# Eight stores of the folded value/output weights, issued from POOL instead of SP

## The chip, the cores and the metric

The kernel runs on one core of one Trainium2 chip. The metric is the device time of one execution in microseconds (us). Besides the timed runs there is one profiled execution, with every instruction and every DMA on record; all quoted rows of the profile come from it. PE is the tensor engine, DVE the vector engine, ACT the scalar engine, POOL the GpSimd engine and SP the sync engine, which here does nothing but issue DMAs.

## The reference

One layer of a streaming encoder on x (2048 tokens x 1024) and mem (256 memory tokens x 1024), all in float32. Cut to what matters:

```python
u = rms_norm(h, g_mix_pre);  z = u @ w_in                  # split into 7 column groups
y = concatenate([swa_with_sinks(...), hgrn2(...)]) @ w_out  # window attention | gated recurrence
h = h + rms_norm(y, g_mix_post)
u = rms_norm(h, g_x_pre);  m = rms_norm(mem, g_mem)
y = cross_attention(u, m, wq_x, wk_x, wv_x, wo_x)           # 4 heads of 256, 256 memory tokens
h = h + rms_norm(y, g_x_post)
u = rms_norm(h, g_ffn_pre)
y = (silu(u @ w_gate) * (u @ w_up)) @ w_down                # 1024 -> 2816 -> 1024
h = h + rms_norm(y, g_ffn_post)
```

## The kernel before

The work runs in three stages, each with pools of its own in SBUF and PSUM.

**Stage 1** projects the first half of the tokens. **Stage 2** projects the second half and runs the window attention and the recurrence. Beside its last part runs `fold_cross` (L285), which folds the cross-attention weights: since the memory is fixed, `wq_x` and the keys are multiplied into one matrix `qk_d`, and the values and `wo_x` into one matrix `vo_d` (1024 x 1024, in DRAM). **Stage 3** (`phases`, L1191) is one long chain of blocked products: the output projection, the scores (with `qk_d`), the values (with `vo_d`), the FFN.

Every product is made in float32 from two halves, "hi" (a rounded copy) and "lo" (the rest), in three matmuls per pair: hi x hi, hi x lo, lo x hi. In stage 3 these are lines L1110, L1111 and L1112, on tiles `S` (stationary, 128x512) and `T` (moving, 128x512 per slice). An `S` tile is made from a raw tile `sraw` that a DMA has loaded: ACT or POOL writes hi (L974, L976), DVE writes lo (L977). Seven products stand in for eight (a Strassen scheme), so DVE also forms sums of raw tiles (`sum`, L1079).

**The end of the fold** is where the change lies (L346 to L369). For each head `h` two tiles of `wo_x` are loaded (`raw`, by SP), split by ACT (`whi`, L150) and DVE (`wlo`, L153), and multiplied on PE (L359 to L361) into four PSUM banks. Then, for each of two row blocks, ACT copies one bank (L366) and DVE another (L367) into the two halves of a row tile `o`, and `o` is stored to `vo_d`: 8 stores of 128x1024 float32, 512 KB each. The tiles `o` come in turn from tag `x` (3 buffers) and tag `z` (2 buffers) of the pool `io` (L61), so the third `z` tile takes the place of the first once that one's store has read it, and the fourth `x` tile that of the first. The names in the rows below are `x_7948`, `x_7996`, `x_8044`, `x_8092` and `z_7952`, `z_8000`, `z_8048`, `z_8096`, in program order.

**What sets the order.** Each engine executes its own instructions strictly in order, and so does each DMA-issuing sequencer: an instruction that waits for a semaphore holds up all that stand behind it on that engine. The order itself is written by a planner at build time, from the program text and its own costs. SP issues nearly all loads and stores, `store` (L77) among them. `store_late` (L80) issues a store from POOL instead; before the change only four stores of stage 1 use it (L652). POOL also issues the accumulating loads of stage 3 (`add`, L1480) and makes some hi halves. The first loads of stage 3 (`sraw` from `y_d`, the output of the two mixers) stand in SP's order behind the stores of the fold.

Of the kernel before, what the change touches and what calls it, by code (L numbers as in the profile page):

```python
# [18 lines left out]
P = 128  # L19
# [29 lines left out]
class Layer:  # L49
# [86 lines left out]
    def raw_tile(self):  # L136
        self._n += 1
        return self.wp.tile([P, D], F32, tag="raw", name=f"raw_{self._n}", bufs=3)

    def split_tiles(self):  # L140
        self._n += 1
        hi = self.wp.tile([P, D], F32R, tag="hi", name=f"whi_{self._n}", bufs=3)
        lo = self.wp.tile([P, D], F32R, tag="lo", name=f"wlo_{self._n}", bufs=3)
        return hi, lo
# [140 lines left out]
    def fold_cross(self):  # L285
# [32 lines left out]
        for d in (0, 4, 1, 5, 2, 6, 3, 7):  # L318
            th, tl = self.wcols(self.I["wq_x"], d, "A")
            o = self.io_tile("x")  # L320
            for q in range(2):
                ps = self.bank("sh"[q])
                for r in range(2):
                    h = 2 * q + r
# [21 lines left out]
        for h in range(4):  # L346
            banks = [[self.bank(k) for k in "sh"] for _ in range(2)]
            for i in range(2):
                j = 2 * h + i
                raw = raw_tile()  # L350
                self.load(raw, self.I["wo_x"][j * P:(j + 1) * P, :])
                wh, wl = split_tiles()
                self.split(raw, wh, wl, "A")
                for mt in range(2):
                    ms = slice(mt * P, (mt + 1) * P)
                    ah, al = vT[0][:, j, ms], vT[1][:, j, ms]
                    for q in range(2):
                        sl = slice(q * 512, (q + 1) * 512)
                        nc.tensor.matmul(banks[mt][q], ah, wh[:, sl], start=(i == 0), stop=False)  # L359
                        nc.tensor.matmul(banks[mt][q], ah, wl[:, sl], start=False, stop=False)  # L360
                        nc.tensor.matmul(banks[mt][q], al, wh[:, sl], start=False, stop=(i == 1))  # L361
                if i == 0:
                    yield
            for mt in range(2):
                o = self.io_tile("xz"[mt])
                nc.scalar.activation(o[:, 0:512], banks[mt][0], AF.Copy)  # L366
                nc.vector.tensor_copy(o[:, 512:D], banks[mt][1])  # L367
                self.store(self.vo_d[(2 * h + mt) * P:(2 * h + mt + 1) * P, :], o)
            yield  # L369


# [1403 lines left out]
```

## Time and profile before

| what | value |
|---|---|
| median of 3 runs | 2562.99 us (2562.63 to 2563.87) |
| profiled execution, its own time | 2559.88 us |
| its span, from the first to the last instruction | 2558.2 us |
| PE busy | 2510.6 us, 98% of the span |
| DVE, ACT, POOL busy | 1758.5, 1248.5, 457.1 us |
| mean clock granted to PE | 0.995 of full speed |
| loads and stores issued by SP (queue q1) | 443.76 MB, 51.7% of the 16 DMA engines' span |
| DMAs issued by POOL (queue q0) | 40.90 MB, 8.4% |
| stores to `vo_d`, issued by SP | 8, between 751.3 and 770.5 us |

How to read the rows: a timeline row has the start in us, the duration, the engine, the line, the operation, output<-input, and in brackets the idle time before it and what ended that. "SPq" is a DMA being issued by SP; the transfer itself comes after it, and "DMA to landing" is the time from issue to the last byte. The windows view has a row per stretch of time: length, busy us of each engine with its count of instructions, the granted clock, the share of the 16 DMA engines in use, and GB/s. A matmul's shown duration is longer than the distance to the next one, since matmuls overlap: the distance from start to start is what counts. Some matmul records are missing from the trace.

### The profile page before, as it was taken

To read this page: it belongs to the slowest core of one execution; us is meant where nothing else is said; L and a number is where in the kernel's file an instruction comes from. 1 tells how busy PE (TensorE), PEld (TensorE's weight loads), DVE (VectorE), ACT (ScalarE), POOL (GpSimd) and SP (SyncE) were. 2 spreads that over 40 slices of the span, in tenths; PEclk is the share of its full clock that TensorE was granted. 3 is DMA by queue.
4 is the path that set the end of the run, shared out by engine and by line. 5 is a ranking of instruction groups with operands and counts; after the bars stand their busy time and mean duration, and the time that the engine had idled before them with its cause. 6 is when DMAs were issued, how large, how long until landed. Compare 5 with 4: busy or idle time off the path is not lost. (4 is left out here: it accounts for less than half of the span.)

```text
span 2558.2 us, 34111 instructions
## 1 busy us (share of the span) xinstructions
PE 2510.6 (98%) x12012; PEld 2095.5 (82%) x12012; DVE 1758.5 (69%) x2813; ACT 1248.5 (49%) x2606; POOL 457.1 (18%) x633
## 2 busy tenths in 40 slices
PE   8999999999998999999999999999999999999998
PEld 7777888887997888888788888888888888888886
DVE  6868587788667578787876555585566666664756
ACT  5454365656654566565554333353333344543543
POOL 2233343222312343224210000000000000000022
PEclk9999999999999999999999999999999999999999
DMA  6254545466986796868973542254555433566798
GB/s 239 98 207 138 174 144 159 152 201 191 286 302 194 229 278 204 278 208 223 312 247 115 181 157 75 93 187 140 181 192 187 165 129 137 202 212 189 228 223 208
DMA packets 269386, 489.97 MB, mean 192 GB/s; under 512 B 20640, under 2 KB 127136, under 8 KB 268704
## 3 DMA queue, kind: packets, MB, share of 16 engines
q1 hardware_dynamic: 256832, 443.76, 51.7%
q0 software_dynamic: 11232, 40.90, 8.4%
q10 hardware_dynamic: 1152, 3.15, 0.3%
q8 instruction: 94, 1.54, 0.2%
q14 instruction: 76, 0.62, 0.1%
HBM read 326.26 MB, written 161.48 MB: 191 GB/s over the span
## 5 line engine op out<-in xcount | busy, mean ns | idle before, releaser
L1110 PE MATMUL psm<-T,S 128*128 128x512 f32 x2744 | 1065.3, 392 | 18.5 <-ACT S L974 9.7
L1111 PE MATMUL psm<-T,S 128*128 128x512 f32 x2744 | 1072.8, 391 | 0.0
L1112 PE MATMUL psm<-T,S 128*128 128x512 f32 x2744 | 1066.0, 391 | 1.9 <-DVE S L977 1.8
L1110 PEld LDWEIGHTS psm<-T,S 128*128 128x128 f32 x2744 | 517.1, 188 | 129.9 <-ACT S L974 10.5
L1112 PEld LDWEIGHTS psm<-T,S 128*128 128x128 f32 x2744 | 516.8, 188 | 111.3 <-DVE S L977 3.7
L1111 PEld LDWEIGHTS psm<-T,S 128*128 128x128 f32 x2744 | 517.2, 188 | 106.4
L974 ACT ACTIVATE S<-sum 128x512 fp32r<-128x512 f32 (+1 forms) x336 | 206.0, 617 | 328.1 <-PE psm L1112 325.0
L977 DVE TENSOR_TENSOR S<-sraw,S 128x512 fp32r<-128x512 f32 (+1 forms) x312 | 211.7, 686 | 218.2 <-ACT S L974 201.8
L977 DVE TENSOR_TENSOR S<-sum,S 128x512 fp32r<-128x512 f32 (+1 forms) x400 | 273.0, 687 | 79.2 <-ACT S L974 64.1
L1125 ACT ACTIVATE part<-psm 128x512 f32<-128x512 f32 x294 | 173.2, 592 | 181.9 <-PE psm L1112 180.8
L974 ACT ACTIVATE S<-sraw 128x512 fp32r<-128x512 f32 (+1 forms) x271 | 165.9, 617 | 168.6 <-PE psm L1112 144.4
L1482 POOL DMA_DIRECT2D row<-y_d x28 | 25.0, 893 | 1070.9 <-DMA sraw<-hid_d 905.3
L1453 ACT ACTIVATE junk<-row 128x512 f32<-128x512 f32 x160 | 99.6, 625 | 97.0 <-DVE row L1475 33.6
L170 PE MATMUL psg<-u,whi 128*128 128x512 f32 x352 | 142.7, 406 | 3.9 <-DVE z L696 2.1
L977 DVE TENSOR_TENSOR T<-row,T 128x1024 fp32r<-128x1024 f32 x104 | 123.0, 1191 | 29.8 <-ACT T L974 29.5
L172 PE MATMUL psg<-u,wlo 128*128 128x512 f32 x352 | 142.0, 403 | 0.5 <-DVE wlo L153 0.5
L171 PE MATMUL psg<-u,whi 128*128 128x512 f32 x352 | 142.0, 403 | 0.0
L974 ACT ACTIVATE T<-row 128x1024 fp32r<-128x1024 f32 x104 | 105.4, 1023 | 24.6 <-DMA row<-in_w_down_dram 9.9
L1657 DVE TENSOR_TENSOR part<-psm,part 128x512 f32<-128x512 f32 x66 | 45.5, 690 | 65.7 <-PE psm L1112 65.6
L976 POOL TENSOR_SCALAR S<-sum 128x512 fp32r<-128x512 f32 x64 | 49.3, 772 | 220.5 <-PE psm L1112 145.2
L153 DVE TENSOR_TENSOR wlo<-raw,whi 128x1024 fp32r<-128x1024 f32 x54 | 68.1, 1263 | 28.5 <-ACT whi L150 18.1
L1648 DVE TENSOR_TENSOR row<-psm,part 128x512 f32<-128x512 f32 x66 | 45.5, 690 | 54.3 <-PE psm L1112 54.2
(341 smaller groups left out, 3465.4 us busy)
## 6 DMA issues: line engine op xcount, KB each, us to landing
sraw<-in_w_gate_dram SPq DMA_DIRECT2D x44, 512.0 KB, 5.1
sraw<-in_w_up_dram SPq DMA_DIRECT2D x44, 512.0 KB, 4.9
hid_d<-row SPq DMA_DIRECT2D x44, 512.0 KB, 2.8
h_d<-row SPq DMA_DIRECT2D x32, 512.0 KB, 6.8
y_d<-row SPq DMA_DIRECT2D x32, 512.0 KB, 3.8
sraw<-hid_d SPq DMA_DIRECT2D x32, 512.0 KB, 5.3
row<-h_d POOLq DMA_DIRECT2D x30, 512.0 KB, 7.3
row<-y_d POOLq DMA_DIRECT2D x28, 512.0 KB, 7.7
```

The lines of the kernel that those rows point to most:

```text
L153: nc.vector.tensor_tensor(lo, raw, f32(hi), ALU.subtract)
L170: nc.tensor.matmul(ps, ah, bh, start=(i == 0), stop=False)
L171: nc.tensor.matmul(ps, ah, bl, start=False, stop=False)
L172: nc.tensor.matmul(ps, al, bh, start=False, stop=(i == n - 1))
L974: self.nc.scalar.activation(hi, raw, AF.Copy)
L976: self.nc.gpsimd.tensor_scalar(hi, raw, 1.0, 1.0, ALU.mult, ALU.mult)
L977: self.nc.vector.tensor_tensor(lo, raw, f32(hi), ALU.subtract)
L1110: nc.tensor.matmul(ps, s[:, 0, k, :], t[:, 0, k, :], start=st, stop=False, **kw)
L1111: nc.tensor.matmul(ps, s[:, 0, k, :], t[:, 1, k, :], start=False, stop=False, **kw)
L1112: nc.tensor.matmul(ps, s[:, 1, k, :], t[:, 0, k, :], start=False, stop=sp, **kw)
L1125: nc.scalar.activation(t, ps, AF.Copy)
L1453: self.nc.scalar.activation(junk, a, AF.Square, scale=float(D) ** -0.5, accum_out=to)
```

## The change

One word changes: the eight stores of the fold are issued by `store_late`, from POOL, instead of `store`, from SP.

```diff
@@ -365,7 +365,7 @@
                 o = self.io_tile("xz"[mt])
                 nc.scalar.activation(o[:, 0:512], banks[mt][0], AF.Copy)
                 nc.vector.tensor_copy(o[:, 512:D], banks[mt][1])
-                self.store(self.vo_d[(2 * h + mt) * P:(2 * h + mt + 1) * P, :], o)
+                self.store_late(self.vo_d[(2 * h + mt) * P:(2 * h + mt + 1) * P, :], o)
             yield
```

The planner's order moves with it, in three places. First, SP at the end of the fold (`raw` are the last loads of `wo_x`, `sraw` the first loads of stage 3); lines with - stood there only before:

```order
-L78 DMA vo_d<-x_7948 128x1024
-L78 DMA vo_d<-z_7952 128x1024
 L75 DMA raw_8056<-in_wo_x_dram 128x1024
 L75 DMA raw_8074<-in_wo_x_dram 128x1024
-L78 DMA vo_d<-x_7996 128x1024
-L78 DMA vo_d<-z_8000 128x1024
-L78 DMA vo_d<-x_8044 128x1024
-L78 DMA vo_d<-z_8048 128x1024
-L78 DMA vo_d<-x_8092 128x1024
 L75 DMA sraw_8118<-y_d 128x2x512
-L78 DMA vo_d<-z_8096 128x1024
 L75 DMA sraw_8120<-y_d 128x2x512
```

Now the loads of stage 3 stand directly behind the last load of `wo_x`, with no store between them.

Second, POOL from the last small operation of the recurrence (L920) to its first work in stage 3 (L976, the hi half of an `S` tile):

```order
 L918 TENSOR_SCALAR h_vv_7698<-h_ss_7692 128x4
 L920 TENSOR_TENSOR h_rs_7700<-h_vv_7698,mhalf 128x4
+L81 DMA vo_d<-x_7948 128x1024
+L81 DMA vo_d<-z_7952 128x1024
+L81 DMA vo_d<-x_7996 128x1024
+L81 DMA vo_d<-z_8000 128x1024
+L81 DMA vo_d<-x_8044 128x1024
+L81 DMA vo_d<-z_8048 128x1024
+L81 DMA vo_d<-x_8092 128x1024
+L81 DMA vo_d<-z_8096 128x1024
 L976 TENSOR_SCALAR S_8199<-sum_8197 128x512
 L976 TENSOR_SCALAR S_8227<-sum_8225 128x512
```

The eight stores stand in a stretch in which POOL had nothing to do, and ahead of its first `S` tile.

Third, ACT at the end of the fold and the start of stage 3, with what each instruction waits for (DMAHW and DMASW are the counters of DMAs issued by SP and by POOL). Before:

```order
L366 ACTIVATE z_8048<-pss_8006 128x512 [waits DMAHW4_49,PE_49]
L150 ACTIVATE whi_8076<-raw_8074 128x1024 [waits DMAHW6_49,DVE_49,PE_49]
L366 ACTIVATE x_8092<-pss_8052 128x512 [waits DMAHW3_49,PE_49]
L366 ACTIVATE z_8096<-pss_8054 128x512 [waits DVE_49,DMAHW0_49,PE_49,Activation_49]
L974 ACTIVATE S_8126<-sraw_8118 128x512 [waits DMAHW4_49,Pool_49]
L974 ACTIVATE S_8129<-sraw_8120 128x512 [waits DMAHW6_49,DVE_49]
L974 ACTIVATE S_8151<-sraw_8122 128x512 [waits DMAHW7_49]
L1125 ACTIVATE part_8149<-psm_8136 128x512 [waits DVE_49,DMAHW3_49,PE_49,Activation_49]
L974 ACTIVATE S_8172<-sraw_8124 128x512 [waits DMAHW0_49]
```

With the change:

```order
L366 ACTIVATE z_8048<-pss_8006 128x512 [waits DMASW5_49,PE_49]
L150 ACTIVATE whi_8076<-raw_8074 128x1024 [waits DMAHW4_49,DVE_49,PE_49]
L366 ACTIVATE x_8092<-pss_8052 128x512 [waits DMASW4_49,PE_49]
L366 ACTIVATE z_8096<-pss_8054 128x512 [waits DVE_49,DMASW7_49,PE_49,Activation_49]
L974 ACTIVATE S_8126<-sraw_8118 128x512 [waits DMAHW5_49,Pool_49]
L974 ACTIVATE S_8129<-sraw_8120 128x512 [waits DMAHW6_49,DVE_49]
L974 ACTIVATE S_8151<-sraw_8122 128x512 [waits DMAHW7_49,DMAHW0_49]
L974 ACTIVATE S_8172<-sraw_8124 128x512 [waits DMAHW0_49]
L1125 ACTIVATE part_8149<-psm_8136 128x512 [waits DVE_49,DMASW2_49,PE_49,Activation_49]
```

The same instructions stand there in nearly the same order. The waits of `z_8048`, `x_8092`, `z_8096` and `part_8149` for a place that a store of the fold still reads are now waits for a store issued by POOL: DMASW5 is the store of `z_7952`, DMASW4 that of `x_7948`, DMASW7 that of `z_8000`, DMASW2 that of `x_8092`. On SP the seventh load of stage 3 (`row_8155`) likewise now waits for the store of `x_8044`. On PE and DVE the instructions of the first blocks of stage 3 (about the first 70 us) change places among each other; none is added or dropped, and behind these blocks the order is as before.

## The prediction

> **What bounds the kernel now.** I read the windows first: how full PE is before, at and behind the place of the change.
>
> ```profile
> 750.00:760.00 10.00, 10.00 (x45) 8.10 (x44) 6.58 (x9) 5.04 (x7) 0.00 (x0) 1.00 0.97 313
> 760.00:770.00 10.00, 9.71 (x42) 7.56 (x40) 4.64 (x7) 4.51 (x6) 0.00 (x0) 1.00 0.52 210
> 770.00:782.00 12.00, 5.61 (x15) 4.43 (x16) 4.15 (x7) 2.28 (x4) 0.98 (x1) 0.72 0.98 334
> 782.00:1259.00 477.00, 475.64 (x2263) 395.74 (x2263) 362.87 (x535) 279.10 (x640) 159.52 (x218) 1.00 0.78 237
> 1270.00:2415.00 1145.00, 1144.68 (x5075) 948.36 (x5073) 724.69 (x1063) 482.68 (x832) 26.68 (x33) 1.00 0.52 169
> ```
>
> The columns after the length are PE, PEld, DVE, ACT, POOL, granted clock, DMA share and GB/s. PE is full in the fold (10.00 of 10), empty for more than half of the 12 us behind it, and full again for nearly the whole of stage 3: 475.64 of 477 us, then 1144.68 of 1145. So PE bounds what follows, and a microsecond that stage 3 starts earlier is nearly a microsecond at the end, since every load, store and split of stage 3 is released by work that moves with it. Next, PE's own rows at the hole, and the waits around it.
>
> ```profile
> 769.32 0.39 PE L361 MATMUL psh<-whi,kv 128*128 128x512 f32 x1
> 776.39 0.80 PE L1110 MATMUL psm<-T,S 128*128 128x512 f32 x1 [6.68 <-ACT S L974]
> 776.98 0.63 PE L1111 MATMUL psm<-T,S 128*128 128x512 f32 x1
> 777.41 0.63 PE L1112 MATMUL psm<-T,S 128*128 128x512 f32 x1
> ...
> 781.13 0.39 PE L1112 MATMUL psm<-T,S 128*128 128x512 f32 x1
> 781.36 0.39 PE L1110 MATMUL psm<-T,S 128*128 128x512 f32 x1
> ```
>
> ```profile
> ACT S L974 <- DMA sraw<-y_d: 8.4, 3, 5.8
> ```
>
> PE ends the fold at 769.71 (769.32 + 0.39) and stands still for 6.68 us, until ACT has made the first `S`; ACT in turn waited for the DMA of `sraw`. Then the clock is low: the matmuls follow each other at 0.43 us (776.98 to 777.41) instead of 0.23 (781.13 to 781.36). The twelve matmuls of the first product thus take 4.97 us, from 776.39 to 781.36; at 0.227 they would take 2.72. Why the DMA is late is seen in SP's queue.
>
> ```profile
> 747.74 0.33 SPq L78 DMA_DIRECT2D y_d<-sg  x1
> ...
> 753.72 0.33 SPq L78 DMA_DIRECT2D vo_d<-z  x1
> 754.80 1.59 SPq L75 DMA_DIRECT2D raw<-in_wo_x_dram  x2
> 758.38 0.33 SPq L78 DMA_DIRECT2D vo_d<-x  x1
> 760.11 0.33 SPq L78 DMA_DIRECT2D vo_d<-z  x1
> 763.73 0.32 SPq L78 DMA_DIRECT2D vo_d<-x  x1
> 764.91 0.32 SPq L78 DMA_DIRECT2D vo_d<-z  x1
> 769.57 0.32 SPq L78 DMA_DIRECT2D vo_d<-x  x1
> 769.99 0.39 SPq L75 DMA_DIRECT2D sraw<-y_d  x1
> 770.50 0.75 SPq L78 DMA_DIRECT2D vo_d<-z  x1
> ```
>
> The last `raw` is issued by 756.39 (754.80 + 1.59). The first `sraw` follows only at 769.99, because five stores stand ahead of it, and each waits until ACT and DVE have copied its tile out of PSUM; the fifth is ready at 769.57. What `sraw` reads was there long before: it is the mixers' output of the first tokens, and even the last store of that output was issued at 747.74. It is a queue held up by its head, not a want of data or of DMA engines (their share is 0.52 in 760 to 770).
>
> **The change part by part.** 1. *SP loses eight stores.* It is free at 756.4, and the six `sraw` loads follow at once, the first about 13 us earlier than now. It needed 5.7 us from issue to ACT's start (769.99 to 775.71, below); even with twice that, 11.4 us, it lands at 768.2, before ACT has any use for it. The six loads are 3 MB; at the 313 GB/s of 750 to 760 they take about 10 us, and with the POOL queue taking half of the engines 20, so the sixth lands between 767 and 777. PE takes the first four at 770.5, 773, 776 and 779 (a product is 12 matmuls, 2.73 us) and the last two in the next block, so neither end makes it wait.
>
> 2. *What is late next.* ACT's first `S` stands behind its last copy of the fold, and DVE's behind its own.
>
> ```profile
> 769.33 0.60 ACT L366 ACTIVATE z<-pss 128x512 f32<-128x512 f32 x1 [0.39 <-PE pss L361]
> 775.71 0.63 ACT L974 ACTIVATE S<-sraw 128x512 fp32r<-128x512 f32 x1 [5.78 <-DMA sraw<-y_d]
> 769.75 0.69 DVE L367 COPY z<-psh 128x512 f32<-128x512 f32 x1 [0.23 <-PE psh L361]
> 776.37 0.69 DVE L977 TENSOR_TENSOR S<-sraw,S 128x512 fp32r<-128x512 f32 x1 [5.93 <-ACT S L974]
> ```
>
> ACT can start the hi half at about 769.8 to 769.9 and ends it at 770.5 (0.63 us); PE starts 0.05 us behind it, as at 776.39. DVE writes lo from 770.5 to 771.2, and PE's third matmul, due at 771.0, waits 0.25 us for it. The hole shrinks from 6.68 to some 0.8 us. Does the clock hold? A hole of 1.21 us elsewhere did not lower it: the matmul behind it is shown with 0.39 us, as at full clock, where a slow one has 0.63.
>
> ```profile
> 2495.81 0.50 PE L1110 MATMUL psm<-T,S 128*128 128x512 f32 x1 [1.21 <-DVE row L1697]
> 2496.15 0.39 PE L1111 MATMUL psm<-T,S 128*128 128x512 f32 x1
> ```
>
> So I take full clock. **The sum**: the first product ends at 770.5 + 2.72 + 0.25 = 773.5 instead of 781.4, a gain of 7.9 us: 5.9 of the hole, 2.25 of the clock, less the 0.25 for lo. The last loads, `row_8155` and on, keep up: they now wait for the store of `x_8044` (ready at 763.73) instead of for SP's turn, and their product is due 8 x 2.73 = 22 us into stage 3.
>
> 3. *POOL gains eight stores.* Nothing of POOL's stands beside them (busy 0.00 of 10 in both windows). The nearest rows are the four stores of the same shape in stage 1, and the accumulating loads of stage 3:
>
> ```profile
> L81 POOL DMA_DIRECT2D z_d<-pair x4: 585/598/807, 207.9 to 257.1; - x4
> DMA to landing us min/median/max: 3.0/3.6/4.2
> ...
> L1482 POOL DMA_DIRECT2D row<-h_d x30: 857/893/1189, 1154.6 to 2543.8; - x30
> DMA to landing us min/median/max: 5.3/7.6/13.0
> ```
>
> 0.6 to 1.2 us of POOL per store, and 3.0 to 13.0 us to landing. I take 0.7 and 5, nearer the rows of the same kind, since the `sraw` loads now run beside them. The last store is issued at 770.5 and off POOL by 771.4; POOL's first `S` needs sums that DVE makes at about 773. Nothing waits: cost 0.
>
> 4. *Tiles come free later.* This is where the cover could fail. The third `z` tile needs the store of the first, the fourth `z` that of the second:
>
> ```profile
> 762.75 0.60 ACT L366 ACTIVATE z<-pss 128x512 f32<-128x512 f32 x1 [0.34 <-PE pss L361]
> 763.45 1.06 ACT L150 ACTIVATE whi<-raw 128x1024 fp32r<-128x1024 f32 x1
> ...
> 766.05 0.40 PE L359 MATMUL pss<-whi,kv 128*128 128x512 f32 x1
> ```
>
> The first store of `z`, issued at 753.72, has 9.0 us to land before the copy at 762.75; behind that copy on ACT stands the last `whi`, ready at 764.5 and due on PE at 766.05, so 1.5 us more are covered. The second (760.11) has 9.2 us before 769.33. `part_8149` waits for the store of `x_8092` (769.57); with 5 us it lands at 774.6, one microsecond behind the end of PE's first product. Behind it on ACT stand `part_8170` and the hi half of `S_8251`, some 1.6 us together; PE wants that one only after four products and four more matmuls, at 770.5 + 0.25 + 10.9 + 0.9 = 782.5. Cost 0 at 5 us; the price of longer landings is the second rival.
>
> 5. *Order.* The planner moves some of PE's matmuls among the first blocks. They need `S` tiles that ACT, DVE and POOL make a few us ahead by the durations above; I take 0, with bounds of -0.5 us and +1.4 us, the whole of PE's idle time in 782 to 1259 (477 less 475.64).
>
> [...]
>
> **The rivals.** *Only issue time is saved (0.12).* If the DMA engines, at 0.97 in 750 to 760, are the limit, the loads merely trade places with the stores: the first `S` is ready when it is now, the time stays 2563. For it: the engines are near full on both sides of the hole, 0.97 and 0.98. Against it: 0.52 between them, and the path needs only the first 512 KB by 770.
>
> *The stores land late (slower, 0.08).* Take L us to landing for every POOL store. Beyond 10.5 the last `whi` delays PE by L - 10.5; the wait of the fourth `z` raises this to L - 9.2; and `S_8251`, ready at 769.57 + L + 1.6 against 782.5 and the 1.4 by which the fourth `z` has moved that, makes PE wait L - 12.7 more. At the longest row, L = 13.0, the loss is 3.8 + 0.3 = 4.1 and the gain 3.8: 2559.2. The gain is gone when 2L = 29.8, at L = 14.9, and the kernel is 0.2% slower from L = 17.5: 2568. For it: POOL's queue shares the engines with six loads. Against it: no POOL row is over 13.0, and the same kind of store took 4.2 at most.
>
> *The change doesn't do what it says*: the order shows the stores on POOL and the loads moved up, so this has no chance of its own.
>
> **How the numbers follow.** The sum was made on the profiled execution, 2559.88 us, of which the span is 2558.2 and 1.7 lies around it; 7.9 us less is 2552.0. The median of the runs is 3.1 us above it; the gain is the same in both: 2562.99 - 7.9 = 2555.1. A measurement of this kernel can tell about 0.2%, 5.1 us, from no change. Chances: the forecast, a gain of 5.1 to 9.5 us, 0.69; more than 9.5, 0.03; stores late enough to leave 3 to 5.1 us, 0.07; the first rival (0.12) and other gains under 3 us, 0.13; slower, 0.08. Faster by over 0.2% is thus 0.72, within 0.2% 0.20, slower 0.08. The range goes from 2553.0 (the hole gone altogether, 9.0 us, and one of noise) to 2561.0, past the L = 13 case, and leaves about 0.19 out: most of the first rival, and slower.
>
> **What would show it.** Right: six `sraw` loads on SP between 756 and 763, the hole of PE at 770 near 0.8 us, 0.23 us between matmuls behind it, the granted clock near 1.00 in that window, POOL's stores at 0.6 to 0.9 us each. Wrong: ACT waiting for a DMA of POOL at its copies of 762 or 769 or at the first `part`, a hole of over 3 us that lowers the clock again, or the same hole with `sraw` landing at 775. Then the gain also may stand at 780 and be given back later, which the holes of PE behind it would tell.

## The result, and the profile after

The changed kernel takes 2554.26 us at the median of six runs (2551.3 to 2558.84); the kernel before took 2563.43 beside it (2562.63 to 2567.0). The ratio is 0.9967 with a 95% interval of 0.9958 to 0.9977: 0.33% faster, or 8.5 us (5.9 to 10.8; 0.0033 x 2563). The forecast was 7.9 us and 2555.1.

First SP's queue in the changed kernel, at the place where the stores stood.

```profile
748.70 7.42 SPq L75 DMA_DIRECT2D raw<-in_wo_x_dram  x4
756.17 3.95 SPq L75 DMA_DIRECT2D sraw<-y_d  x6
```

All six `sraw` loads are issued from 756.17, where the first of them had to wait until 769.99. Next PE around the end of the fold, and ACT beside it.

```profile
768.85 0.40 PE L361 MATMUL psh<-whi,kv 128*128 128x512 f32 x1
770.04 0.50 PE L1110 MATMUL psm<-T,S 128*128 128x512 f32 x1 [0.79 <-ACT S L974]
770.37 0.40 PE L1111 MATMUL psm<-T,S 128*128 128x512 f32 x1
770.76 0.50 PE L1112 MATMUL psm<-T,S 128*128 128x512 f32 x1
...
773.17 0.39 PE L1110 MATMUL psm<-T,S 128*128 128x512 f32 x1
```

```profile
768.87 0.60 ACT L366 ACTIVATE z<-pss 128x512 f32<-128x512 f32 x1 [0.36 <-PE pss L361]
769.36 1.66 ACT L974 ACTIVATE S<-sraw 128x512 fp32r<-128x512 f32 x3
772.40 0.64 ACT L974 ACTIVATE S<-sraw 128x512 fp32r<-128x512 f32 x1 [1.38 <-DMA sraw<-y_d]
776.00 1.09 ACT L1125 ACTIVATE part<-psm 128x512 f32<-128x512 f32 x2 [2.96 <-DVE sum L1079]
```

The hole is 0.79 us instead of 6.68. ACT makes the first `S` right behind its last copy of the fold, without a wait for a DMA. The thirteenth matmul (773.17) comes 3.13 us behind the first (770.04) instead of 4.97, so the clock has held. The windows of the same execution (columns as in the prediction) show the same stretch from further off.

```profile
760.00:770.00 10.00, 9.25 (x41) 7.25 (x39) 5.04 (x6) 4.93 (x8) 2.02 (x4) 1.00 1.00 373
770.00:782.00 12.00, 11.96 (x51) 9.61 (x52) 10.15 (x16) 5.57 (x10) 2.89 (x5) 1.00 1.04 409
```

PE is busy for 11.96 of the 12 us behind the fold, where it was busy for 5.61, and the DMA engines are now full from 760 to 770 (1.00, before 0.52): the loads use the time in which SP's queue stood still.

### The profile page after: what moved, and what is told of

Same layout as the page of the kernel before. It is cut to its first block, busy times and chain, and to the rows that moved or that the text cites. A ratio compares the mean times of both kernels' runs of the same rounds, so it can differ in the third digit from the quotient of the medians.

```text
span 2551.7 us, 34118 instructions
## 1 busy us (share of the span) xinstructions
PE 2508.4 (98%) x12012; PEld 2091.8 (82%) x12012; DVE 1759.2 (69%) x2813; ACT 1250.0 (49%) x2606; POOL 465.4 (18%) x641
## 4 chain that ended last, share of the span: by engine, by line
PE 89%; DMA 3%; DVE 2%; issue 2%; ACT 2%; POOL 1%; SPq 0%; POOLq 0%; DVEq 0%; ACTq 0%
PE psm L1110 23%; PE psm L1112 23%; PE psm L1111 23%; PE psg L170 3%; PE psg L172 3%; PE psg L171 3%; PE pss L1364 1%; DMA row<-h_d 1%; PE pss L824 0%; PE pst L824 0%; DMA sraw<-y_d 0%; PE psh L870 0%; PE psh L170 0%; PE psh L171 0%; PE psh L172 0%
## 5 line engine op out<-in xcount | busy, mean ns | idle before, releaser
L976 POOL TENSOR_SCALAR S<-sum 128x512 fp32r<-128x512 f32 x64 | 52.1, 814 | 174.1 <-PE psm L1112 142.4
```

What stands on the lines that cost most here:

```text
L976: self.nc.gpsimd.tensor_scalar(hi, raw, 1.0, 1.0, ALU.mult, ALU.mult)
```

## The experiments

The diffs below are shortened; `...` stands for what is left out. For the runs of the table one number tells what happened at the place of the change: the time from the start of the fold's last matmul to the thirteenth matmul of stage 3, that is the hole and the first product together. Before it is 781.36 - 769.32 = 12.04 us; in the changed kernel 773.17 - 768.85 = 4.32, so 7.72 are saved there. The gains in the last column are (1 - ratio) x 2562, with their intervals.

| kernel | hole, us | fold to 13th matmul, us | saved there, us | gain in time, us |
|---|---|---|---|---|
| changed: all 8 stores on POOL | 0.79 | 4.32 | 7.72 | 8.5 (5.9 to 10.8) |
| last 4 on POOL | 0.79 | 4.32 | 7.72 | 9.0 (5.6 to 12.0) |
| first 4 on POOL | 6.91 | 12.59 | -0.55 | -0.8 (-3.3 to 2.1) |
| last 2 on POOL | 2.25 | 5.76 | 6.28 | 5.4 (3.3 to 7.7) |
| all on SP, loads first | 0.79 | 4.34 | 7.70 | 7.4 (4.4 to 10.5) |
| all 8 on ACT | 1.93 | 5.47 | 6.57 | 8.2 (4.9 to 11.3) |
| changed, stores doubled | 4.25 | 9.94 | 2.10 | 0.0 (-2.6 to 2.3) |

**Which stores matter: the last four.**

```diff
-                self.store(self.vo_d[...], o)
+                (self.store_late if h >= 2 else self.store)(self.vo_d[...], o)
```

> The stores of heads 0 and 1 (four) stay on SP, those of heads 2 and 3 (four) go to POOL. Theory (SP is held up at its head): the last store left on SP is ready at 760.1, so the six sraw loads are issued from about 760.5, land ahead of 769, and the hole of PE is 0.8 us as with all eight moved: a gain of 7.5 to 9 us, 2554 to 2556. Rival (bytes: what counts is how much is taken off SP's queue, or how much of the loads' time is freed): four of eight stores give half, 4 to 5 us, 2559. Rival (only issue time saved): four issues of 0.33 us, at most 1.3 us, 2562 to 2563.

The time was 2553.63 us, ratio 0.9965 (0.9953 to 0.9978). SP's queue in this run:

```profile
758.46 0.33 SPq L78 DMA_DIRECT2D vo_d<-z  x1
758.84 4.82 SPq L75 DMA_DIRECT2D sraw<-y_d  x6
```

Half of the stores bring the whole gain. The loads wait for the fourth store instead of the seventh, and that is early enough.

**The mirror image: the first four.**

```diff
+                (self.store_late if h < 2 else self.store)(self.vo_d[...], o)
```

> The mirror image: heads 0 and 1 on POOL, heads 2 and 3 on SP, so the number of stores and bytes on each queue is that of the run with the last four. Theory: SP still has the store that is ready at 769.57 ahead of the first sraw load, so sraw is issued at 770, the hole stays at 6.7 us with the low clock behind it, and the time is that of the kernel before, 2562.5 to 2564. Rival (bytes): half of the gain, 4 to 5 us, 2559. The POOL stores here run beside no sraw load: if those loads are what lengthened the landings (7.1 us at the median in the changed kernel, against 5 assumed), they land in about 4 us.

2562.55 us, ratio 1.0003 (0.9992 to 1.0013). SP's queue, PE's first matmul of stage 3, and the landing of the four POOL stores:

```profile
768.35 0.32 SPq L78 DMA_DIRECT2D vo_d<-x  x1
768.76 0.39 SPq L75 DMA_DIRECT2D sraw<-y_d  x1
```

```profile
775.38 0.80 PE L1110 MATMUL psm<-T,S 128*128 128x512 f32 x1 [6.91 <-ACT S L974]
```

```profile
DMA to landing us min/median/max: 3.1/4.1/5.1
```

The same number of stores and bytes has left SP, and nothing is gained: one store that waits for its data ahead of the loads is enough to hold them (768.35, and the first load at 768.76). The two runs together rule out both rivals that count stores: "half for half" wanted 4 to 5 us from each, "only issue time" at most 1.3. The 1.3 us are four issues of 0.33 us each. The run with the first four stays within them (-0.8 us), the one with the last four does not (9.0): what the second issuer saves there is SP's wait, not its issue time.

**A smaller dose: the last two.**

```diff
+                (self.store_late if h == 3 else self.store)(self.vo_d[...], o)
```

> Only the two stores of head 3 go to POOL, six stay on SP. Theory: the last store ahead of the first sraw load is then the one ready at 764.9, so sraw is issued at about 765.3 and, with 5.7 us to ACT's start, S begins at 771.0 and ends at 771.6: a hole of 1.9 us, 1.1 more than in the changed kernel, still too short to lower the clock (a hole of 1.21 us did not): a gain of 6.5 to 7.5 us with a quarter of the stores moved, 2556 to 2557. Rival (bytes): a quarter of the gain, 2 us, 2561. Rival (issue time): 0.7 us, 2563. If 1.9 us lower the clock, the gain is 4.5 to 5.5 us.

2556.53 us, ratio 0.9979 (0.9970 to 0.9987). SP's queue, and PE's first matmul of stage 3:

```profile
766.55 0.32 SPq L78 DMA_DIRECT2D vo_d<-z  x1
766.96 4.15 SPq L75 DMA_DIRECT2D sraw<-y_d  x6
```

```profile
773.50 0.50 PE L1110 MATMUL psm<-T,S 128*128 128x512 f32 x1 [2.25 <-ACT S L974]
```

The loads follow the sixth store, and PE starts 6.54 us after the first of them is issued (766.96 to 773.50). A quarter of the stores brings 6.28 us at the place, a little under the expected 6.5 to 7.5, since the hole is 2.25 us and not 1.9; the time shows 5.4, with an interval that includes both. The clock held behind this hole of 2.25 us; behind one of 2.22 us, in the run with 24 matmuls below, it did not.

**No POOL store at all.** The four stores of heads 2 and 3 stay on SP, but an order without a wait puts them behind the first four `sraw` loads.

```diff
+                next(phases)              # issues the first loads of stage 3
+                loads = ...               # those on SP
+                for st in self.held_back: # the stores with h >= 2
+                    tc.add_manual_dep(st, loads[-1].name, ... NoSync ..., reason="issue_after")
```

> No store goes to POOL. On SP the four stores of heads 2 and 3 are put behind the first four sraw loads; nothing else of the change is made. Theory: sraw is issued from about 760.5, the hole shrinks to 0.8 us and the gain is that of the change, 7.5 to 9 us, 2554 to 2556; the fifth and sixth load follow at about 771 and are wanted only in the next block, so they cost nothing. The stores keep SP's shorter landings (4 to 5 us). Rival (a second queue is what brings it: loads and stores must run from two issuers): no gain, 2563, or at most 1 us.

2554.97 us, ratio 0.9971 (0.9959 to 0.9983). SP's queue:

```profile
762.85 0.33 SPq L78 DMA_DIRECT2D vo_d<-z  x1
763.23 2.56 SPq L75 DMA_DIRECT2D sraw<-y_d  x4
...
773.96 1.61 SPq L75 DMA_DIRECT2D sraw<-y_d  x2
```

Four loads are issued behind the fourth store, two behind the eighth, and the hole is again 0.79 us. A second queue is not what brings the gain; the order in one queue does as much.

**Another issuer: ACT.**

```diff
-                self.store(self.vo_d[...], o)
+                self.put(self.vo_d[...], o)       # nc.scalar.dma_start
```

> All eight stores are issued by ACT. Theory: any queue other than SP frees the sraw loads, so most of the gain is there; but ACT now waits in its own order for DVE's half of each tile, and the last two stores (ready at 769.6 and 770.5, 0.33 us each) stand ahead of its first S: that S ends at about 771.5 instead of 770.5, the hole is about 1.8 us and the gain 6.5 to 7.5 us, 2556 to 2557. Rival (POOL's queue itself brings it): no gain, 2563. If the waits also held up the copies of PSUM and the whi behind them so that PE stood inside the fold, the gain would be under 4 us, 2559 or more.

2554.02 us, ratio 0.9968 (0.9956 to 0.9981). ACT's instructions, and the stores that it issues (ACTq):

```profile
768.36 0.33 ACTq L84 DMA_DIRECT2D vo_d<-x  x1
769.28 0.33 ACTq L84 DMA_DIRECT2D vo_d<-z  x1
769.71 1.15 ACT L974 ACTIVATE S<-sraw 128x512 fp32r<-128x512 f32 x2 [1.07 <-DVE z L367]
```

POOL is not needed either. The price is the expected one: ACT waits 1.07 us for DVE's half of `z` before it may issue the last store, and the hole is 1.93 instead of 0.79. That 1.1 us is seen in the trace; the times cannot tell it.

**The clock's share of the sum.** The kernel before, with matmuls that nobody reads behind the fold, so that PE does not stand still while `sraw` is still late.

```diff
+            if h == 3:
+                ps = self.bank("g")
+                ...                       # behind the fold's last matmul
+                for r in range(24):
+                    nc.tensor.matmul(ps, vT[0][:, 7, 0:P], wh[:, 0:512], start=(r == 0), stop=(r == 23))
```

> The kernel before with 24 more matmuls of 128x512 behind the last one of the fold, into a PSUM bank that nobody reads: work that the kernel does not need, 24 x 0.23 = 5.5 us, so PE is busy until about 775.2 while the first S is still ready at 776.4. The stores stay on SP. Theory (the sum has two terms, 5.9 us of hole and 2.25 us of clock): only the clock's part is gained, since the remaining hole is about 1.1 us: the first product at 0.23 us a matmul, 2.0 to 2.3 us faster, about 2561. Rival (the low clock behind the hole comes from elsewhere, not from PE's idle time): matmuls at 0.43 us as before, 2563.

2563.22 us, ratio 0.9999 (0.9991 to 1.0008): nothing gained. SP's queue and PE tell why:

```profile
773.07 0.32 SPq L78 DMA_DIRECT2D vo_d<-z  x1
773.48 3.60 SPq L75 DMA_DIRECT2D sraw<-y_d  x5
```

```profile
772.12 5.66 PE L369 MATMUL psg<-whi,kv 128*128 128x512 f32 x24
779.99 0.80 PE L1116 MATMUL psm<-T,S 128*128 128x512 f32 x1 [2.22 <-ACT S L980]
780.59 0.63 PE L1117 MATMUL psm<-T,S 128*128 128x512 f32 x1
```

The planner had put the eighth store ahead of the first load as well, so `S` came about a microsecond later than before: PE's first product starts 8.10 us behind the start of the fold's last matmul (0.23 us ahead of 772.12) instead of 7.07 (769.32 to 776.39). A hole of 2.22 us was left, and the clock behind it was low: the next matmul follows after 0.60 us instead of 0.33, and is shown with 0.63 instead of 0.40. The run said nothing on the question and was made again, with 28 matmuls and SP's order as before:

> The run with 24 dummy matmuls did not test what it should: there both last stores stood ahead of the first sraw load (one of them behind it in the kernel before), so S came 1.2 us later, the hole left was 2.2 us and the clock was low all the same. Here 28 dummy matmuls (again work that the kernel does not need, nobody reads them) follow the fold, 28 x 0.236 = 6.6 us, and the last store is held behind the first sraw load, so SP's order is that of the kernel before. Theory: PE stands still for less than 0.6 us ahead of the first product, its matmuls follow each other at 0.23 us, and 2.0 to 2.3 us are gained, about 2560; the trace decides, since the times tell 2.5 us apart at best. Rival (the low clock comes whatever PE does ahead): 0.43 us a matmul, 2562.

2559.21 us, ratio 0.9982 (0.9972 to 0.9991), a gain of 4.6 us (2.3 to 7.2). PE, from the 28 matmuls to the thirteenth of stage 3:

```profile
770.61 6.58 PE L376 MATMUL psg<-whi,kv 128*128 128x512 f32 x28
777.62 0.51 PE L1125 MATMUL psm<-T,S 128*128 128x512 f32 x1 [0.43 <-ACT S L989]
...
780.75 0.39 PE L1125 MATMUL psm<-T,S 128*128 128x512 f32 x1
```

With PE kept busy the first product takes 3.13 us (777.62 to 780.75) as in the changed kernel, though `S` is as late as before. So the low clock does come from PE's idle time, and its share is 4.97 - 3.13 = 1.84 us. The gain in time is larger than that 1.84, and the lower end of its interval, 2.3, is also above it; where the rest comes from was not traced.

**The cover of the tile slots.** The changed kernel, each store issued twice:

```diff
+                self.store_late(self.vo_d[...], o)
+                self.store_late(self.vo_d2[...], o)
```

> The changed kernel with each of the eight POOL stores issued twice, the second copy to another DRAM tile that nobody reads: 4 MB of work that the kernel does not need. It tests the cover of the tile slots: a slot comes free when its second copy has landed. Theory (cover up to L = 9.2 and 10.5 us, then PE waits): with L about 10 to 11 the loss against the changed kernel is 0 to 2 us, 2554 to 2557; with L about 14 it is 3.5 to 5 us, 2558 to 2560, with ACT waiting for a DMA of POOL at its copies of 762 or 769 or at its first part. Rival (the slots never matter within such lengths): 2554 whatever L is, and no wait of ACT for the stores.

2561.13 us, ratio 1.0000 (0.9991 to 1.0010): the whole gain is gone. ACT, then PE, then the landing of the stores:

```profile
767.47 0.60 ACT L367 ACTIVATE z<-pss 128x512 f32<-128x512 f32 x1 [1.80 <-DMA vo_d<-z]
...
775.86 0.60 ACT L367 ACTIVATE z<-pss 128x512 f32<-128x512 f32 x1 [3.83 <-DMA vo_d<-z]
...
787.59 1.09 ACT L1127 ACTIVATE part<-psm 128x512 f32<-128x512 f32 x2 [5.82 <-DMA vo_d<-x]
```

```profile
777.03 0.80 PE L1112 MATMUL psm<-T,S 128*128 128x512 f32 x1 [4.25 <-ACT S L976]
```

```profile
DMA to landing us min/median/max: 5.2/11.2/14.7
```

ACT waits for stores at the two copies of `z` and at the first `part` (its copy of a finished product of stage 3 out of PSUM), the three places that the prediction named, and the wait at the second copy makes PE's hole 4.25 us, which lowers the clock again. The time is over the 2558 to 2560 expected for long landings: the first product behind the hole takes 5.29 us instead of 3.13, and the expectation had not counted the low clock. But it could still be the 4 MB as such. So the third `z` got a tile of its own, with the bytes unchanged:

```diff
-                o = self.io_tile("xz"[mt])
+                o = self.io.tile([P, D], F32, tag="zf", ..., bufs=1) if (h, mt) == (2, 1) else self.io_tile("xz"[mt])
```

> The run with every store doubled (second copy to a DRAM tile that nobody reads, 4 MB more), with one more tile of its own for the third z, so that neither the third nor the fourth z waits for a store that was issued less than 15 us before. The bytes and POOL's work are those of the doubled run. Theory (tile slots): ACT's waits of 1.8 and 3.8 us ahead of its copies of z are gone, S follows the fold at once, the hole falls from 4.25 to 0.8 us and the clock holds: 5 to 6 us less than the doubled run's 2561.1, that is 2555 to 2556, or up to 2558 if the wait of the first part for the last x (5.8 us of ACT) now costs PE more. Rival (it is the 4 MB through the same DMA engines that cost the time): 2560 to 2562.

2562.08 us, ratio 0.9997 (0.9988 to 1.0005): not the gain that was expected. PE and ACT:

```profile
771.46 0.50 PE L1112 MATMUL psm<-T,S 128*128 128x512 f32 x1 [0.75 <-ACT S L976]
...
788.83 0.80 PE L1112 MATMUL psm<-T,S 128*128 128x512 f32 x1 [4.01 <-ACT S L976]
```

```profile
786.13 1.08 ACT L1127 ACTIVATE part<-psm 128x512 f32<-128x512 f32 x2 [5.58 <-DMA vo_d<-x]
```

The hole at the fold closed as the theory says, from 4.25 to 0.75 us. But the wait only moved: the first `part` lies in the place of the last `x` and waits 5.58 us for that store, and 17 us into stage 3 PE has a hole of 4.01 us with the low clock behind it. My expectation had taken PE to lose at most 2 to 3 us there. In the last run this one store is issued only once:

```diff
+                if (h, mt) != (3, 0):
+                    self.store_late(self.vo_d2[...], o)
```

> The run with the extra slot closed the hole at the fold (0.75 us) and opened one of 4.0 us with a low clock 17 us later, behind ACT's wait of 5.6 us for the store of the last x, ahead of the first part, whose tile lies in the place of that x. Here that one store is issued once, the other seven stay doubled (3.5 MB more instead of 4, work that the kernel does not need). Theory (tile slots, and the wait merely moved from z to part): the last x lands at about 781 to 783, the wait of part falls from 5.6 us to 1 to 2.5 and the hole behind it from 4.0 to 0 to 1 us with the clock held: 2555 to 2557.5. Rival (the bytes cost the time): seven eighths of the loss stay, 2561.

2559.49 us, ratio 0.9985 (0.9976 to 0.9994): 3.8 us (1.5 to 6.1) under the kernel before. POOL's last store of `x` with its landing (that of this one store), ACT's first `part`, PE, and a stretch behind PE's second row (columns as in the prediction):

```profile
769.60 0.53 POOL L81 DMA_DIRECT2D vo_d<-x  x1 [3.24 <-ACT z L367]
...
DMA to landing us min/median/max: 12.6/12.6/12.6
```

```profile
782.34 1.09 ACT L1128 ACTIVATE part<-psm 128x512 f32<-128x512 f32 x2 [3.34 <-PE psm L1115]
```

```profile
770.01 0.50 PE L1113 MATMUL psm<-T,S 128*128 128x512 f32 x1 [0.74 <-ACT S L977]
...
785.04 0.50 PE L1113 MATMUL psm<-T,S 128*128 128x512 f32 x1 [1.79 <-ACT S L977]
```

```profile
787.21:790.62 3.41, 3.41 (x10) 2.65 (x9) 3.41 (x6) 3.41 (x7) 0.41 (x1) 0.50 1.07 406
```

`part` now starts 12.3 us behind PE's first product (770.01 to 782.34) instead of 14.7 (771.46 to 786.13), 2.3 us earlier, and the hole shrinks by nearly as much, from 4.01 to 1.79. The row names PE as releaser, but the store lands at 782.2 (769.60 + 12.6), just ahead of `part`, and in the run before the same instruction names the store. So it is the landing of single stores at single slots that sets the holes. The bytes count through the landings: a single store that stands behind doubled ones on POOL's queue still took 12.6 us, where the same store, issued at 769.58, takes 6.3 in the changed kernel. The landing was in time, within the expected 781 to 783; what failed in this expectation is what follows from it. The hole is 1.79 us instead of at most 1, and the clock did not hold: it was at 0.50 from 787.21 to 790.62. So 2555 to 2557.5 was not reached. At the place the sum comes out: 7.77 us saved at the fold (773.14 - 768.87 = 4.27 there), less 0.28, 1.79 and 0.35 of holes in the next 20 us and an estimated 1.7 for 3.41 us at half the clock, leaves about 3.65, and the time shows 3.8.

## Why the prediction was right, point by point

**1. SP freed: right.** The six loads follow the last `raw` at 756.17, 13.8 us earlier than before. They were in time: the first landed after 7.2 us, at 763.4 (the prediction's bound, 756.4 + 11.4, is 767.8, not 768.2), and ACT's first three `S` run without a break. Only the fourth load came late, by 1.38 us of ACT's time, and PE did not feel it. That the held-up head is the cause, and not the number of stores, their bytes or the second issuer, is shown by the runs with the first and the last four stores and by the one with the loads put first on SP.

**2. The next thing late: right.** The forecast was a hole of some 0.8 us behind ACT's last copy, the clock held, and 0.25 us for lo. The hole is 0.79 us, 5.89 less (forecast 5.9), and the first product takes 1.84 us less (forecast 2.25 - 0.25 = 2.00; its first three matmuls follow at 0.33, 0.39 and, to the fourth, 0.34 us instead of 0.23). The sum there is 7.73 us against 7.9. Behind a hole of 0.79 us the clock held in all three kernels of the table that have one (4.32, 4.32 and 4.34 us from the fold to the thirteenth matmul).

The profiled pair differs by less, 2558.2 - 2551.7 = 6.5 us of span. Such differences occur between executions without any change there: the hole before the matmul at 2409.49 is 1.63 us after and 0.97 before, but 1.40 in the run with the first four stores and 1.48 in the one with 24 dummies, neither of which gained anything. PE's rows show some of the rest: holes of 0.33 and 0.31 us at 880 and 882, which the execution before does not have, and 1.59 us instead of 0.93 ahead of the first matmul of L1364 at 1239. The runs with more repeats (8.5 us, interval 5.9 to 10.8) do not tell 7.9 from 6.5.

**3. POOL's cost: right in the result, the landing too short.** A store takes POOL 0.53 us, less than the 0.7 assumed, and nothing waits for POOL. But the landing is 5.2 to 7.9 us, median 7.1, instead of 5:

```profile
L81 POOL DMA_DIRECT2D vo_d<-x x4: 533/533/657, 751.6 to 769.6; - x4
L81 POOL DMA_DIRECT2D vo_d<-z x4: 533/533/539, 754.0 to 770.5; - x4
...
DMA to landing us min/median/max: 5.2/7.1/7.9
```

The loads beside them go with it: four such stores from POOL ahead of the loads landed in 3.1 to 5.1 us, as the run with the first four shows, and the four that ran with the loads in 6.5 to 9.0 (the run with the last four). In the changed kernel itself the two stores issued ahead of the first `sraw` landed in 5.3 and 5.2 us, the six behind it in 6.3 to 7.9.

**4. Tile slots: right, with less room than thought.** The changed kernel is inside the cover, and the doubled run shows the waits where they were named. At the fourth `z` the cover is 8.5 us and not 9.2: the second store of `z` is issued at 760.34 and ACT copies at 768.87. It landed in 7.6 us, so 0.9 us were left. At `part` ACT starts at 776.00, just behind the landing of the last `x` (769.58 + 6.3 = 775.9), but PE wanted what follows only later. For this place the prediction let PE wait from L = 12.7, of which 1.4 us come from a late fourth `z` that holds PE itself. Without that its terms give 782.5 - 1.6 - 769.57 = 11.3 us, and the last run, in which no `z` waits, measures 11.0: PE wanted its operand at 785.04 - 1.79 = 783.25, and it was there 2.70 us after `part` started (782.34 to 785.04), so `part` may start as late as 780.55, that is 10.95 us behind the issue at 769.60. The 1.6 us from `part` to `S` are 2.7 in that run, whose order has a `junk` row (the squares for a norm) between them on ACT. In the changed kernel's order none stands there, and `S` ends at 777.60, 1.6 us behind 776.00, as predicted.

**5. Order: nothing that shows.** DVE's rows of line 1475, matched one by one between two profiled executions, start 7.9 us earlier after the change than before at 879 us, and 6.7 at 913. This looks like the planner's reorder giving something back. But the run with the last four stores, which has the very same order on PE, DVE and ACT, leads by 9.0 at 879 and 8.9 at 935, and the run with the first four, which gains nothing, also falls back against before, from 0.5 at 879 to -0.4 at 995. So the loss is not clearly the order's; its bounds of -0.5 and +1.4 us were not tested by a run of their own.

**The rivals.** "Only issue time" is refuted by the pair of runs above. "The stores land late" did not happen, but the mechanism exists: with doubled stores it took the whole gain. It reached 2561, no more than before.

## What to carry to other kernels

SP's queue issued its first `sraw` at 769.99, behind a store that was ready only at 769.57, though the data of the load had been there long before. So ask of every load that is late not only when its data exist but what stands ahead of it and what that waits for. Moving the stores that waited last to another queue (all eight to POOL or ACT, the last four or two to POOL), or the last four behind the loads in the same one, gave 5 to 9 us here, and moving the four early ones gave nothing. Then check how long the moved stores take to land and who next uses their tiles, since a slot that stays occupied can turn the gain into a wait somewhere else: with doubled stores (landing in 11.2 us at the median, 7.1 in the changed kernel) ACT waited 3.83 us for one and the gain was 0.0. Removing that wait at one slot only showed the next, 5.58 us at `part`.

## What the runs showed of the hardware

The length of a hole of PE did not by itself tell whether its clock dropped. The same hole in stage 2, ahead of the same matmul, was 2.07 us in the kernel before and in the changed one, where the clock stayed at 1.00 behind it, and 2.06 us in the run with the last two stores on POOL, where it was at 0.50. The two holes at the change agree: 2.25 us with the clock held (last two on POOL), 2.22 us with it lost (24 dummies).

The granted clock on record shows more. Its drops to 0.50, but for one at the end of each trace, lasted 3.41 or 6.83 us. In the kernel before they began at 149.51, 248.49, 774.14 and 1262.25 us, which are 29, 154 and 143 steps of 3.413 us apart; in the changed one at 149.11, 248.09 and 1258.44, 29 and 296 steps apart. Cut into stretches of 3.413 us on these times, from 13 us on, where the record of the clock begins, the two traces agree: where PE stood still for 1.02 to 1.45 us of a stretch at full clock, the next was at full clock in all ten cases; where it stood still for 1.98 us or more, the next was at 0.50 in all nine; none lay between. So in these two traces the drops went with the idle time within one such stretch, and not with the length of a hole. The hole in stage 2 shows it, first in the changed kernel, then in the run with the last two stores on POOL (a row of PE, then two windows, columns as in the prediction):

```profile
604.53 0.50 PE L170 MATMUL psg<-u,whi 128*128 128x512 f32 x1 [2.07 <-DVE z L696]
```

```profile
603.08:606.49 3.41, 1.96 (x8) 1.62 (x9) 3.41 (x8) 0.01 (x1) 0.00 (x0) 1.00 1.12 261
606.49:609.91 3.42, 3.42 (x17) 2.76 (x16) 3.42 (x9) 0.42 (x2) 0.00 (x0) 1.00 1.03 401
```

```profile
605.04 0.51 PE L170 MATMUL psg<-u,whi 128*128 128x512 f32 x1 [2.06 <-DVE z L696]
```

```profile
602.08:605.49 3.41, 1.34 (x7) 0.81 (x6) 3.41 (x6) 0.93 (x2) 0.00 (x0) 1.00 1.03 208
605.49:608.90 3.41, 3.41 (x10) 2.63 (x9) 3.41 (x8) 0.00 (x0) 0.00 (x0) 0.50 1.10 365
```

In the first the hole lies across the border of two stretches, with 1.45 us in the second (3.41 - 1.96); in the other all of its 2.06 us lie in one. A shorter hole came with a drop too: one of 1.83 us at 247 us before (1.84 in the changed kernel) lay in a stretch with 2.35 us idle in all (1.98), and the next was at 0.50 in both; the one of 1.79 us in the run with the last `x` issued once was followed by 0.50 from 787.21. So were the longer holes: 6.68 us (before), 4.25 (stores doubled) and 4.01 (extra slot) with slow matmuls behind them, and one of 3.78 us at 148 us before. The holes of 0.79 us at the change were not. Of the 2.25 us in the run with the last two, 1.48 lay in one stretch and 0.76 in the next, counted on from the drop at 605.49. So a hole of about 2 us cost here either its own length or, by an estimate from the drop, some 1.7 us more (half of 3.41); that this spreads the times of one kernel was not tested. How the chip itself measures this was not shown.
